# The first pair of modulation channels computed one block of 128 at a time, with the first key and value products between the two

## The chip, the cores and the metric

The kernel runs on one core of a Trainium2 chip. The metric is device time in microseconds (us) of one execution. TensorE (PE in the profile) multiplies and transposes, VectorE (DVE) and ScalarE (ACT) do elementwise work, GpSimd (POOL) a few small powers, and SyncE (SP) issues most of the loads.

## The reference

Two layers run over 256 latent tokens `x` and 256 context tokens `ctx`, each token 2048 channels wide. What matters here is how the first layer begins:

```python
shift, scale, gate = adaln(c, ada_w[i], ada_b[i])        # silu(c) @ w + b, in three
h  = modulate(rms_norm(x, norm_g[i]), shift[:, None], scale[:, None])
shift_c, scale_c, gate_c = adaln(c_ctx, ada_w[i], ada_b[i])
hc = modulate(rms_norm(ctx, norm_g[i]), shift_c, scale_c)   # h * (1 + scale) + shift
...
p  = h @ w_in                                            # queries, keys, values, ...
pc = hc @ w_in[:, base:]
```

So the first projection needs, for each channel, a scale and a shift that come from a matrix-vector product with `ada_w` (2048 rows), and the normalised tokens with the channel on the partitions. Attention, a state-space scan, an output projection and a second layer follow; the change does not touch them.

## The kernel before

Everything stays in float32 accuracy by splitting operands in a high and a low part: each product of a token block with a weight block is three matmuls (high by high, low by high, high by low). `hH[kb]` and `hL[kb]` are the high and low part of the modulated tokens for channel block `kb` (128 channels, 512 tokens: x in the first 256, ctx in the others); there are 16 such blocks. `w0` holds the weights of keys, values and queries in segments of 256 channels by 512 columns, 512 KB each. A weight segment lands in a `raw` buffer, ACT casts it to its high part, DVE subtracts to make the low part.

The first projection runs over eight pairs of channel blocks, `j` = 0 to 7. For each pair:

- `ada_gen` makes the scale (`A0`) and the shift (`S0`) of its 256 channels. Each needs four 512 KB blocks of `ada0` (512 rows by 256 columns each). PE multiplies them with `cpad`, which holds the two conditioning vectors in 32 columns, so that four row groups can stand in four strips of a PSUM bank (`32 * g`). ACT copies the bank to `half` (L724), PE turns it (L199), DVE sums the strips (L732) and adds the bias (L735, L736, L738).
- Then ACT makes `hH` (L757) and DVE a full-precision copy (L759) and from it `hL` (L763).
- The main loop multiplies: K and V for four token tiles of 128, Q for two, and one further block of 256 columns (`b_part`).

The tokens come in rows: `x_load(t)` loads tile t in two transfers (L583), `x_norm` squares, sums and scales it (L601, L603, L613, L615), `x_pair` turns two channel blocks by four transposes of 128 by 128 (L199) and copies them out on ACT and DVE (L628, L629) to `xm`. Tiles 0 and 1 are x, tiles 2 and 3 ctx. Tile 2 is loaded into the buffer of tile 0 (tag `KT`) and tile 3 into that of tile 1 (tag `KL`).

Order is set twice. Loads go through one list (`loads`) in the order in which it was filled, each as soon as a buffer is free, all on SP's queue: nine 512 KB buffers at the start. Instructions are recorded by a planner: `ada_gen`, `x_gen(0)` and `x_gen(1)` are generators that yield what they wait for, `pump` and `force` take the one that the planner's own clock finds ready, and the main loop calls them between its matmuls. Each engine then runs its instructions in the order of recording. For `j` = 0 the weights of K are split by halves of 128 channels (`split_half`, L440 and L443), and the main loop runs K for both token tiles of x, channel block 0 first, then V, then Q, and the ctx tiles 2 and 3 after them.

```python
q_ada(0)                 # 8 blocks: scale and shift of channel blocks 0 and 1
w_seg(0, CK, CV, CQ)     # K, V, Q weights of the pair
loads.append(lambda: x_load(2))
loads.append(lambda: x_load(3))
```

Of the kernel before, what the change touches and what calls it, by code (L numbers as in the profile page):

```python
# [14 lines left out]
D = 2048  # L15
# [126 lines left out]
def kernel(ctx: ExitStack, tc, x, cx, ada0, w0, adaT, w_in, w_out, sc_in, sc_out, rpb, small, const,  # L142
# [12 lines left out]
    def st(shape, tag, dt=F32, name=None):  # L155
        return sb.tile(list(shape), dt, tag=tag, name=name or tag, bufs=1)
# [15 lines left out]


    xrow = [st([128, D], "KT", name="x0")]
    QT, Vt, gt = st([128, 4, 256], "QT", F32R), st([128, 4, 512], "Vt"), st([128, 4, 256], "gt")
    xrow.append(st([128, D], "KL", name="x1"))
    QL = st([128, 4, 256], "QL", F32R)
# [219 lines left out]
    def place():  # L397
        in_use.append(free_w.popleft())
        return in_use[-1]
# [36 lines left out]
    def split_half(b):  # L436

        raw, v = RAW[0]
        H, Lo = (w[0].rearrange("p (b c) -> p b c", b=2) for w in (WH, WL))
        E(S.copy(H[:, b], v[:, b]))  # L440

        def rest():
            E(V.tensor_tensor(out=Lo[:, b], in0=v[:, b], in1=H[:, b].bitcast(F32), op=ALU.subtract))  # L443
            if b:
                RAW.pop(0)
                place()
                HL[0] = (H, Lo)
                pos["split"] += 1
                give_raw(raw)
                issue()  # L450

        halfsplit.append(rest)

# [79 lines left out]
    loads.append(lambda: E(DMA.dma_start(sm[:, NFIRST:], small[:, NFIRST:])))  # L533
    loads.append(lambda: E(DMA.dma_start(cs_[:, CFIRST:], const[:, CFIRST:])))
    weight(w_in, 0, 2, COL_B, 256)
    q_ada(1)
    for j in range(1, 8):
        w_seg(j, CK, CV)
        if j < 7:
            q_ada(j + 1)  # L540
        w_seg(j, CQ)
        weight(w_in, j * 256, 2, COL_B, 256)
    loads.append(later_loads)

    order = list(range(0, 6)) + list(range(8, 16)) + [6, 7]
# [32 lines left out]
    def x_load(t):  # L578
        src = x if t < 2 else cx
        r0 = (t % 2) * 128  # L580
        xt = xrow[t] if t < 2 else st([128, D], ("KT", "KL")[t % 2], name=f"x{t}")
        for q in range(0, 4, 2):
            E(DMA.dma_start(xt[:, q * 512:(q + 2) * 512], src[r0:r0 + 128, q * 512:(q + 2) * 512]))  # L583
            XS[4 * t + q], XS[4 * t + q + 1] = (xt[:, p * 512:(p + 1) * 512] for p in (q, q + 1))

    x_load(0)
    x_load(1)
# [112 lines left out]
    need = [0]  # L700

    def ada_gen():
        bc = lambda ap: ap.unsqueeze(2).to_broadcast([128, 2, 2])
        for j in range(8):
            k2 = slice(2 * j, 2 * j + 2)
            for part, dst in ((0, A0), (1, S0)):
                ps = None
                for q in range(4):
                    key = ("ada", j, part, q)
                    w_ = 2 if j == 0 else 4  # L710
                    if q % w_ == 0:
                        ks = [("ada", j, part, q + i) for i in range(w_)]
                        yield when(lambda: all(k in RAW for k in ks))
                        yield W_("PE", *[RAW[k][1] for k in ks], nb=0 if ps is not None else 1)
                    if ps is None:
                        ps = bank()
                    raw, v = RAW.pop(key)
                    for g in range(4):
                        mm(ps[32 * g:32 * g + 32, :256], cpad[:, 4 * q + g, :], v[:, g, :], q == 0, q == 3)
                    give_raw(raw)  # L720
                    issue()
                yield W_("ACT", ps)
                Rt = half()
                E(S.copy(Rt, ps[:, :256]))  # L724

                yield W_("PE", Rt)
                for b in range(2):
                    turn(ps[:, 256 + b * 128:384 + b * 128], Rt[:, b * 128:(b + 1) * 128])
                give(free_h, Rt)
                yield W_("DVE", ps)  # L730
                p2 = dst[:, k2, :]
                E(V.tensor_reduce(out=p2, in_=ps[:, 256:].rearrange("p (b g c) -> p b c g", b=2, c=32)[:, :, 0:2, :],  # L732
                                  axis=AX.X, op=ALU.add))
                if part == 0:
                    E(V.tensor_tensor(out=dst[:, k2, :], in0=p2, in1=bc(bs1[:, k2]), op=ALU.add))  # L735
                    E(V.tensor_tensor(out=dst[:, k2, :], in0=dst[:, k2, :], in1=bc(g0[:, k2]), op=ALU.mult))  # L736
                else:
                    E(V.tensor_tensor(out=dst[:, k2, :], in0=p2, in1=bc(P_("ab0")[:, k2]), op=ALU.add))  # L738
                give(free_b, ps)

            for ts in ((0, 1), (2,), (3,)) if j == 0 else ((0, 1, 2, 3),):
                yield when(lambda: all(("xm", t, j) in got for t in ts))
                spans = [(k, slice(max(256 * k, 128 * ts[0]), min(256 * k + 256, 128 * ts[-1] + 128)))
                         for k in range(2) if {2 * k, 2 * k + 1} & set(ts)]
                o = slice(128 * ts[0], 128 * ts[-1] + 128)
                for kb in (2 * j, 2 * j + 1):
                    if j:

                        yield when(lambda: need[0] >= j or plan.t["DVE"] <= plan.t["PE"] + 600)
                    yield W_("DVE", xnT[kb][:, o])  # L750
                    hf = tmp()
                    if hH[kb] is None:
                        hH[kb] = st([128, 512], f"hH{kb}", F32R, name=f"hH{kb}")
                    if ts == (0, 1):
                        split_half(kb)
                    for k, ok_ in spans:
                        E(S.activation(hH[kb][:, ok_], xnT[kb][:, ok_], AF.Identity, scale=A0[:, kb, k:k + 1],  # L757
                                       bias=S0[:, kb, k:k + 1]))
                        E(V.tensor_scalar(out=hf[:, ok_], in0=xnT[kb][:, ok_], scalar1=A0[:, kb, k:k + 1],  # L759
                                          scalar2=S0[:, kb, k:k + 1], op0=ALU.mult, op1=ALU.add))  # L760
                    if hL[kb] is None:
                        hL[kb] = st([128, 512], f"hL{kb}", F32R, name=f"hL{kb}")
                    E(V.tensor_tensor(out=hL[kb][:, o], in0=hf[:, o], in1=hH[kb][:, o].bitcast(F32), op=ALU.subtract))  # L763
                    give(free_t, hf)
                    if ts == (0, 1):
                        halfsplit.pop()()
                if ts == (0, 1):
                    hold[0] = False
                    split()
                    split()  # L770
                got.update(("h", j, t) for t in ts)


    Bl, Cl = st([128, 2, 256], "Bl"), st([128, 2, 256], "Cl")
# [94 lines left out]

    for j in range(8):  # L870
        need[0] = j
        force(lambda: ("h", j, 0 if j == 0 else 3) in got, (urgent,))
        if j == 0:

            w3 = [use(k) for k in range(3)]
            psQ = banks(2)
            psk = banks(2)
            for k in range(2):

                for i, (a_, w_) in enumerate(((hH, 0), (hL, 0), (hH, 1))):  # L880
                    for t in range(2):
                        mm(psk[t], a_[k][:, t * 128:(t + 1) * 128], w3[0][w_][:, k], k == 0 and i == 0, k == 1 and i == 2)
            for t in range(2):
                spawn(urgent, part_gen(j, "K", t, parK[t], psk[t]))
            pump()
            for t in range(2):
                kv(j, "V", t, w3[1])
# [25 lines left out]
    force(lambda: all(("part", 7, key, t) in got for key in "KV" for t in range(4)), (urgent,))  # L913
    got.add(("V", 0))
    KT, KL = st([128, 4, 512], "KT", F32R), st([128, 4, 512], "KL", F32R)


    cwh = st([128, 160], "cwh")
# [1134 lines left out]
```

## Time and profile before

| what | us |
|---|---|
| median of three runs | 1763.31 |
| the runs | 1763.47, 1763.31, 1760.44 |
| profiled execution | 1760.31 |
| its span in the profile | 1758.5 |
| PE busy in the span | 1736.7 |
| DVE busy, ACT busy | 1223.6, 773.4 |

The profile is one execution. Its span runs from the first to the last recorded instruction; 1.8 us of the execution's own time lie around it. A matmul on float32 data (the transposes apart) stands in the trace as two instructions; those on split operands (fp32r) as one.

### The profile page before, as it was taken

Reading aid. Unit: us, or ns where it says so; the run is one execution under the profiler, and the core shown is the slowest. Engines: PE = TensorE matmul, PEld = TensorE weight load, DVE = VectorE, ACT = ScalarE, POOL = GpSimd, SP = SyncE. Lnnn points to the kernel's source line nnn. Section 1 sums busy time; section 2 is a strip of 40 time slices with the busy share of each in tenths; the row PEclk is TensorE's granted clock in tenths of the full one; section 3 lists DMA queues with packets and bytes.
Section 4 is the critical chain, followed back from the end, with each engine's and each line's share of the span. In section 5 each row is a group of like instructions: output and inputs, shape, how many; then the busy total and the mean of one; then the engine's idle time right before and its main releaser. Section 6 shows DMA issues by size and latency. Waiting matters only on the chain.

```text
span 1758.5 us, 25025 instructions
## 1 busy us (share of the span) xinstructions
PE 1736.7 (99%) x9451; PEld 1463.1 (83%) x9451; DVE 1223.6 (70%) x1978; ACT 773.4 (44%) x1330; POOL 31.6 (2%) x28
## 2 busy tenths in 40 slices
PE   6999999999999999999999999999999999999998
PEld 4777988889888889888888898888888888888887
DVE  5666887878685878686877787787668555555554
ACT  5333544445242436343435343564446444444442
POOL 0000100001000000000000000000000000000000
PEclk9999999999999999999999999999999999999999
DMA  9987644686756767656776557768767666666563
GB/s 362 342 307 258 209 143 138 183 246 191 234 165 195 219 205 227 210 175 210 220 213 193 166 185 255 246 221 284 274 222 228 195 188 192 192 191 188 190 208 121
DMA packets 202536, 377.66 MB, mean 215 GB/s; under 512 B 32384, under 2 KB 69040, under 8 KB 202416
## 3 DMA queue, kind: packets, MB, share of 16 engines
q1 hardware_dynamic: 195152, 369.49, 65.5%
q10 hardware_dynamic: 7264, 6.58, 1.1%
q8 instruction: 74, 1.21, 0.3%
q14 instruction: 46, 0.38, 0.1%
HBM read 370.62 MB, written 6.71 MB: 215 GB/s over the span
## 4 chain that ended last, share of the span: by engine, by line
PE 94%; DMA 2%; DVE 2%; issue 1%; ACT 0%; POOL 0%; SPq 0%; ACTq 0%; DVEq 0%; POOLq 0%
PE bank L195 91%; PE bank L199 3%; DMA tmp<-dram_csr 1%; DVE w L427 1%; DMA raw<-in_ada 0%; DMA tmp<-dram_exr 0%; DMA raw<-in_adaT 0%; DVE tmp L1235 0%; ACT w L420 0%; POOL statk L572 0%; DVE mix L1562 0%; SPq L583 0%; DVE raw L823 0%; DVE tmp L603 0%; DVE Vt L1012 0%
## 5 line engine op out<-in xcount | busy, mean ns | idle before, releaser
L420 ACT CAST w<-raw 128x1024 fp32r<-128x1024 f32 x343 | 359.5, 1049 | 530.4 <-PE bank L195 447.7
L427 DVE TENSOR_TENSOR w<-raw,w 128x1024 fp32r<-128x1024 f32 x343 | 416.6, 1217 | 231.4 <-ACT w L420 230.1
L195 PE MATMUL bank<-hH,w 128*128 128x256 f32 (+1 forms) x2064 | 488.0, 324 | 1.2 <-DVE w L427 1.1
L195 PE MATMUL bank<-w,hH 128*128 128x512 f32 x1280 | 407.4, 396 | 2.7 <-ACT hH L757 2.5
L195 PEld LDWEIGHTS bank<-hH,w 128*128 128x128 f32 x2064 | 344.7, 188 | 34.2 <-DVE w L427 2.1
L195 PE MATMUL bank<-hL,w 128*128 128x256 f32 (+1 forms) x1040 | 334.3, 321 | 0.0
L195 PEld LDWEIGHTS bank<-w,hH 128*128 128x128 f32 x1280 | 237.7, 189 | 54.4 <-issue 4.0
L195 PE MATMUL bank<-w,hL 128*128 128x512 f32 x640 | 249.9, 391 | 0.1
L195 PEld LDWEIGHTS bank<-hL,w 128*128 128x128 f32 x1040 | 196.3, 189 | 14.9
L195 PE MATMUL bank<-w,h 128*128 128x512 f32 x768 | 179.7, 390 | 0.0
L823 DVE CUSTOM_DVE_ANT_0 raw<-raw,csb 128x1024 f32<-128x1024 f32 x128 | 155.4, 1219 | 26.2 <-DMA raw<-in_adaT 24.0
L195 PEld LDWEIGHTS bank<-w,h 128*128 128x128 f32 x768 | 143.6, 188 | 29.6
L195 PEld LDWEIGHTS bank<-w,hL 128*128 128x128 f32 x640 | 120.5, 188 | 25.4 <-DVE hL L763 0.6
L195 PE MATMUL bank<-w,mix 128*128 128x512 f32 x588 | 138.3, 391 | 0.9 <-DVE w L427 0.9
L195 PEld LDWEIGHTS bank<-w,mix 128*128 128x128 f32 x588 | 109.5, 188 | 24.0 <-DVE w L427 1.3
L1235 DVE SCALAR_TENSOR_TENSOR tmp<-bank,cwh,tmp 128x508 f32<-128x508 f32 (+1 forms) x96 | 71.0, 744 | 1.8
L195 PE MATMUL bank<-KL,h 128*128 128x512 f32 x264 | 63.8, 389 | 0.0
L427 DVE TENSOR_TENSOR KL<-raw,KL 128x1024 fp32r<-128x1024 f32 x32 | 39.1, 1223 | 33.1 <-ACT KL L420 33.1
L427 DVE TENSOR_TENSOR wL<-raw,wH 128x1024 fp32r<-128x1024 f32 x31 | 37.9, 1224 | 33.5 <-ACT wH L420 33.4
L427 DVE TENSOR_TENSOR QL<-raw,QT 128x1024 fp32r<-128x1024 f32 x32 | 39.2, 1224 | 29.8 <-ACT QT L420 29.8
L195 PEld LDWEIGHTS bank<-KL,h 128*128 128x128 f32 x264 | 49.5, 188 | 10.2
L195 PE MATMUL bank<-QT,h 128*128 128x512 f32 x168 | 56.2, 391 | 0.0
(291 smaller groups left out, 1984.7 us busy)
## 6 DMA issues: line engine op xcount, KB each, us to landing
raw<-in_w_in SPq DMA_DIRECT2D x196, 512.0 KB, 3.9
raw<-in_adaT SPq DMA_DIRECT2D x128, 512.0 KB, 4.8
raw<-in_sc_in SPq DMA_DIRECT2D x128, 512.0 KB, 3.8
raw<-in_w_out SPq DMA_DIRECT2D x64, 512.0 KB, 5.0
raw<-in_ada SPq DMA_DIRECT2D x34, 512.0 KB, 6.9
raw<-in_sc_out SPq DMA_DIRECT2D x32, 512.0 KB, 4.1
PT<-in_ada SPq DMA_DIRECT2D x16, 512.0 KB, 6.9
raw<-in_w SPq DMA_DIRECT2D x16, 512.0 KB, 6.1
```

What stands on the lines that cost most here:

```text
L195: E(T.matmul(o, l, r, start=start, stop=stop, skip_group_check=True))
L199: E(T.transpose(o, i, ident if k == 128 else ident[:k, :k]))
L420: E(S.copy(H, v))
L427: E(V.tensor_tensor(out=Lo, in0=v, in1=H.bitcast(F32), op=ALU.subtract))
L823: E(V.tensor_tensor_reduce(out=raw, in0=raw, in1=csb, scale=1.0, scalar=0.0, op0=ALU.mult, op1=ALU.add, accum_out=gp[:, h, m:m + 1]))
L1235: E(V.scalar_tensor_tensor(out=do, in0=di, scalar=cwh[:, 32 * k + ch:32 * k + ch + 1], in1=do, op0=ALU.mult, op1=ALU.add))
```

## The change

1. `ada0` is repacked on the host for the first pair: eight blocks of 512 KB as before, each now 1024 rows by 128 columns. A scale or a shift of 128 channels then needs two blocks.
2. The load order becomes: four blocks for channel block 0, K and V weights, four blocks for channel block 1, Q weights, tiles 2 and 3. Two small loads (the rest of `small` and `const`) go from behind tile 3 to the end of the first projection's list.
3. `ada_gen` computes scale and shift of channel block 0 alone, makes its `hH`, `hL` and the first half of the K weights, and reports `("row", 0)`; then the same for channel block 1.
4. The main loop runs K and then V with channel block 0 for both token tiles of x, waits for channel block 1, and runs K and V with it. Q follows as before.
5. `x_gen(0)` turns the first two channel blocks of x and then waits until the first K products are recorded (`k0`) before it turns the other fourteen.
6. Tile 2 gets buffers of its own (`QT` and `QL`, not yet in use then). Tile 3 now waits for the buffer of tile 0.

In the recorded order of the changed kernel, PE's instructions from the first one on are: scale of block 0 (8 + 8 matmuls of 128 columns), 4 transposes, one turn, shift of block 0 (8 + 8), one turn, K with block 0 (6), 28 transposes, scale of block 1 (8 + 8), V with block 0 (6), one turn, shift of block 1 (8 + 8), one turn, a small turn, K and V with block 1 (12), Q (12), and then tile 2.

```diff
-    q_ada(0)
-    w_seg(0, CK, CV, CQ)
+    def q_ada_one(kb):
+        for part in range(2):
+            for q in range(2):
+                loads.append(("a", ("one", kb, part, q), ada0, 4 * kb + 2 * part + q, 8, 0, 128, 2))
+
+    q_ada_one(0)
+    w_seg(0, CK, CV)
+    q_ada_one(1)
+    w_seg(0, CQ)
     loads.append(lambda: x_load(2))
     loads.append(lambda: x_load(3))
-    loads.append(lambda: E(DMA.dma_start(sm[:, NFIRST:], small[:, NFIRST:])))
-    loads.append(lambda: E(DMA.dma_start(cs_[:, CFIRST:], const[:, CFIRST:])))
...
-        xt = xrow[t] if t < 2 else st([128, D], ("KT", "KL")[t % 2], name=f"x{t}")
+        xt = xrow[t] if t < 2 else None if t == 2 else st([128, D], "KT", name="x3")
...
         for k2 in range(c, KB // 2):
+            if k2 == 1 and not c:
+                yield when(lambda: "k0" in got)
             yield from x_pair(k2, ts)
...
+        def part_sum(part, kbs, keys, together):
+            n = 128 * len(kbs)
+            nb, ps = 1024 // n, None
+            for q in range(len(keys)):
...
+                for g in range(nb):
+                    ki = q * nb + g
+                    mm(ps[32 * (g % 4):32 * (g % 4) + 32, :n], cpad[:, ki, :], v[:, g, :], ki < 4, ki >= 12)
...
+        for kb in range(2):
+            for part in range(2):
+                yield from part_sum(part, (kb,), [("one", kb, part, q) for q in range(2)], 1)
+            yield both((0, 1), 0)
+            yield from rows_of(0, kb, (0, 1))
+            got.add(("row", kb))
+            if kb == 0:
+                split()
...
-        force(lambda: ("h", j, 0 if j == 0 else 3) in got, (urgent,))
+        force(lambda: ("h", j, 3) in got if j else ("row", 0) in got, (urgent,))
         if j == 0:
+            w3, pss0 = [], []
+            for k in range(2):
+                if k:
+                    force(lambda: ("h", 0, 1) in got, (urgent,))
+                for q, (key, par) in enumerate((("K", parK), ("V", parV))):
+                    if k == 0:
+                        w3.append(use(q))
+                        pss0.append(banks(2))
+                    for i, (a_, w_) in enumerate(((hH, 0), (hL, 0), (hH, 1))):
+                        for t in range(2):
+                            mm(pss0[q][t], a_[k][:, t * 128:(t + 1) * 128], w3[q][w_][:, k], k == 0 and i == 0, k == 1 and i == 2)
+                    got.add("k0")
+                    pump()
...
```

More of the change, by code (lines that the diff above doesn't have):

```diff
@@ L445, in rest @@
                 RAW.pop(0)
+                give_raw(raw)
+                issue()
+            else:
                 place()
@@ L542 @@
         weight(w_in, j * 256, 2, COL_B, 256)
+    loads.append(lambda: E(DMA.dma_start(sm[:, NFIRST:], small[:, NFIRST:])))
+    loads.append(lambda: E(DMA.dma_start(cs_[:, CFIRST:], const[:, CFIRST:])))
     loads.append(later_loads)
@@ L580, in x_load @@
         r0 = (t % 2) * 128
[L581 removed]
+        xt = xrow[t] if t < 2 else None if t == 2 else st([128, D], "KT", name="x3")
         for q in range(0, 4, 2):
[L583 to L584 removed]
+            xq = xhalf[q // 2] if xt is None else xt[:, q * 512:(q + 2) * 512]
+            E(DMA.dma_start(xq, src[r0:r0 + 128, q * 512:(q + 2) * 512]))
+            XS[4 * t + q], XS[4 * t + q + 1] = xq[:, :512], xq[:, 512:]
     x_load(0)
@@ L702, in ada_gen @@
     def ada_gen():
[L703 to L771, printed above, removed]
@@ new lines, in part_sum @@
+        def part_sum(part, kbs, keys, together):
+            n = 128 * len(kbs)
+            nb, ps = 1024 // n, None
+            for q in range(len(keys)):
+                if q % together == 0:
+                    ks = keys[q:q + together]
+                    yield when(lambda: all(k in RAW for k in ks))
+                    yield W_("PE", *[RAW[k][1] for k in ks], nb=0 if ps is not None else 1)
+                if ps is None:
+                    ps = bank()
+                raw, v = RAW.pop(keys[q])
+                for g in range(nb):
+                    ki = q * nb + g
+                    mm(ps[32 * (g % 4):32 * (g % 4) + 32, :n], cpad[:, ki, :], v[:, g, :], ki < 4, ki >= 12)
+                give_raw(raw)
+                issue()
+            yield W_("ACT", ps)
+            Rt = half()
+            E(S.copy(Rt[:, :n], ps[:, :n]))
+            yield W_("PE", Rt)
+            for b in range(len(kbs)):
+                turn(ps[:, 256 + b * 128:384 + b * 128], Rt[:, b * 128:(b + 1) * 128])
+            give(free_h, Rt)
+            yield W_("DVE", ps)
+            k2 = slice(kbs[0], kbs[-1] + 1)
+            dst = (S0 if part else A0)[:, k2, :]
+            bc = lambda ap: ap[:, k2].unsqueeze(2).to_broadcast([128, len(kbs), 2])
+            E(V.tensor_reduce(out=dst, in_=ps[:, 256:256 + n].rearrange("p (b g c) -> p b c g", b=len(kbs), c=32)[:, :, 0:2, :],
+                              axis=AX.X, op=ALU.add))
+            if part == 0:
+                E(V.tensor_tensor(out=dst, in0=dst, in1=bc(bs1), op=ALU.add))
+                E(V.tensor_tensor(out=dst, in0=dst, in1=bc(g0), op=ALU.mult))
+            else:
+                E(V.tensor_tensor(out=dst, in0=dst, in1=bc(P_("ab0")), op=ALU.add))
+            give(free_b, ps)
@@ new lines, in rows_of @@
+        def rows_of(j, kb, ts):
+            spans = [(k, slice(max(256 * k, 128 * ts[0]), min(256 * k + 256, 128 * ts[-1] + 128)))
+                     for k in range(2) if {2 * k, 2 * k + 1} & set(ts)]
+            o = slice(128 * ts[0], 128 * ts[-1] + 128)
+            if j:
+                yield when(lambda: need[0] >= j or plan.t["DVE"] <= plan.t["PE"] + 600)
+            yield W_("DVE", xnT[kb][:, o])
+            hf = tmp()
+            if hH[kb] is None:
+                hH[kb] = st([128, 512], f"hH{kb}", F32R, name=f"hH{kb}")
+            if ts == (0, 1):
+                split_half(kb)
+            for k, ok_ in spans:
+                E(S.activation(hH[kb][:, ok_], xnT[kb][:, ok_], AF.Identity, scale=A0[:, kb, k:k + 1],
+                               bias=S0[:, kb, k:k + 1]))
+                E(V.tensor_scalar(out=hf[:, ok_], in0=xnT[kb][:, ok_], scalar1=A0[:, kb, k:k + 1],
+                                  scalar2=S0[:, kb, k:k + 1], op0=ALU.mult, op1=ALU.add))
+            if hL[kb] is None:
+                hL[kb] = st([128, 512], f"hL{kb}", F32R, name=f"hL{kb}")
+            E(V.tensor_tensor(out=hL[kb][:, o], in0=hf[:, o], in1=hH[kb][:, o].bitcast(F32), op=ALU.subtract))
+            give(free_t, hf)
+            if ts == (0, 1):
+                halfsplit.pop()()
@@ new lines, in ada_gen @@
+        both = lambda ts, j: when(lambda: all(("xm", t, j) in got for t in ts))
+        for kb in range(2):
[6 more added lines that the diff above has]
+                split()
+        hold[0] = False
+        split()
+        got.update(("h", 0, t) for t in (0, 1))
+        for t in (2, 3):
+            yield both((t,), 0)
+            for kb in range(2):
+                yield from rows_of(0, kb, (t,))
+            got.add(("h", 0, t))
@@ L774 @@
+        for j in range(1, 8):
+            for part in range(2):
+                yield from part_sum(part, (2 * j, 2 * j + 1), [("ada", j, part, q) for q in range(4)], 4)
+            yield both((0, 1, 2, 3), j)
+            for kb in (2 * j, 2 * j + 1):
+                yield from rows_of(j, kb, (0, 1, 2, 3))
+            got.update(("h", j, t) for t in range(4))
     Bl, Cl = st([128, 2, 256], "Bl"), st([128, 2, 256], "Cl")
@@ L2028 @@
                      for j in range(8) for b in (2048, 0) for q in range(4)]).reshape(64, 128, 1024)
+    for kb in range(2):
+        for part, b in enumerate((2048, 0)):
+            for q in range(2):
+                w = f('ada_w')[0][q * 1024:(q + 1) * 1024, b + kb * 128:b + kb * 128 + 128]
+                ada0[4 * kb + 2 * part + q] = w.reshape(8, 128, 128).transpose(1, 0, 2).reshape(128, 1024)
     w0 = np.stack([f('na_ssd_w_in')[0][j * 256:j * 256 + 256, c:c + 512].reshape(2, 128, 512).transpose(1, 0, 2)
```

24 lines of the change are left out of this document (9 added, 15 removed).

## The prediction

> **What bounds the kernel now.** I read the page's head first, then what PE waited for after the first 40 us, then PE's busy time and granted clock in stretches (columns of a stretch: its bounds, its length, PE busy and instructions, clock, DMA share, GB/s).
>
> ```profile
> span 1758.5 us, 25025 instructions
> PE 1736.7 (99%) x9451; PEld 1463.1 (83%) x9451; DVE 1223.6 (70%) x1978; ACT 773.4 (44%) x1330; POOL 31.6 (2%) x28
> ```
>
> ```profile
> PE bank L195 <- DVE w L427: 2.0, 3, 0.9
> PE bank L199 <- POOL r L1664: 0.3, 1, 0.3
> PE bank L195 <- DVE gt L789: 0.2, 1, 0.2
> ```
>
> ```profile
> 17.39:21.23 3.84, 3.31 (x51) 1.00 1.03 410
> 21.23:24.64 3.41, 1.84 (x8) 1.00 1.03 406
> 24.64:28.05 3.41, 3.41 (x9) 0.50 1.02 403
> 28.05:31.46 3.41, 3.41 (x16) 1.00 1.06 395
> 31.46:34.87 3.41, 2.32 (x12) 1.00 1.03 406
> 34.87:38.28 3.41, 3.06 (x12) 1.00 1.03 412
> ```
>
> After 40 us PE waits 2.5 us in 1718. Whatever comes after the start is a fixed amount of PE work, and the recorded order of the changed kernel is the same there apart from the first few pairs. So the change is worth what it moves the moment at which PE goes over to unbroken work. In the stretches up to 24.64 PE is idle for 0.53 and 1.57 us, and from 24.64 to 28.05 it runs at half clock, which loses half of 3.41, 1.7 us. These 3.8 us are all that lies between the first transposes and the last matmul of queries, so no more than this can be won. DMA runs at about 400 GB/s all the while, but the next rows show that PE, not a landing, sets this stretch.
>
> ```profile
> 10.82 2.28 PE L195 MATMUL bank<-raw,cpad 128*32 128x256 f32 x16 [10.82 <-DMA raw<-in_ada]
> 13.03 4.36 PE L199 MATMUL bank<-const,x 128*128 128x128 f32 x32
> 17.32 1.07 PE L195 MATMUL bank<-raw,cpad 128*32 128x256 f32 x16
> 20.57 0.61 PE L195 MATMUL bank<-xtm,cpad 128*32 128x256 f32 x8
> 23.35 0.74 PE L195 MATMUL bank<-w,hH 128*128 128x512 f32 x2 [1.11 <-ACT hH L757]
> ```
>
> ```profile
> 12.02 0.20 PEld L195 LDWEIGHTS bank<-raw,cpad 128*32 128x32 f32 x8 [0.99 <-DMA raw<-in_ada]
> 10.00:15.00 5.00, 4.06 (x28) 2.40 (x29) 2.12 (x7) 2.88 (x8) 0.56 (x1) 1.00 1.03 417
> ```
>
> The first two blocks of the scale are waited for (10.82 and 12.02). At 417 GB/s a block of 524288 bytes takes 1.26 us, so block n lands at about 10.8 + 1.26 (n - 1). By then PE is in the 32 transposes, and from 17.32 on it finds its blocks there. The last shift matmul ends at 20.57 + 0.61 = 21.18, the first K matmul starts at 23.35.
>
> ```profile
> 23.35 10.21 PE bank L195 x36
> 33.56 0.23 PE bank L199 x2
> ```
>
> This is the chain of waits. K, V and Q of the x tiles, 36 matmuls, take 10.21 us and end at 33.56; tile 2 follows. 33.56 is the mark that I compare.
>
> **The change, step by step.** The new order is worked through from 13.03, where the first four transposes start in both.
>
> *Up to the first K.* Shift of channel block 0 needs block 4: 10.8 + 3 x 1.26 = 14.6, and half of the 1.07 us that two blocks took, 15.15. From there the way to K is that of before, 23.35 - 21.18 = 2.17:
>
> ```profile
> 21.25 0.37 ACT L724 COPY half<-bank 128x256 f32<-128x256 f32 x1 [2.42 <-PE bank L195]
> 21.68 0.44 PE L199 MATMUL bank<-const,half 128*128 128x128 f32 x2 [0.49 <-ACT half L724]
> 23.33 0.43 DVE L763 TENSOR_TENSOR hL<-tmp,hH 128x256 fp32r<-128x256 f32 x1 [0.28 <-ACT hH L757]
> 23.67 0.68 DVE L443 TENSOR_TENSOR w<-yi,w 128x512 fp32r<-128x512 f32 x1
> 28.38 0.63 PE L195 MATMUL bank<-w,hH 128*128 128x512 f32 x2
> 33.17 0.39 PE L195 MATMUL bank<-w,hH 128*128 128x512 f32 x1
> 33.81 0.27 ACT L628 COPY xm<-bank 128x128 f32<-128x128 f32 x1 [1.58 <-PE bank L199]
> ```
>
> The copy is half as wide (0.27 for 0.37) and one turn of the two falls away, so 2.0: K starts at 17.15, 6.2 us before now. Its weights are block 5, 15.85, and their cast fits in before `hH`. K's last two matmuls want the low part of the weights, which ends 1.0 us after K's first start (23.67 + 0.68 - 23.35). A matmul costs 0.228 us (21 start between 28.38 and 33.17, with the clock at 1.00 but for the first instants), so K with block 0 ends at 17.15 + 1.0 + 0.45 = 18.6.
>
> *The 28 transposes that now follow.* On ACT and DVE their copies go so:
>
> ```profile
> 14.81 2.99 ACT L628 COPY xm<-bank 128x256 f32<-128x256 f32 x7 [0.25 <-PE bank L199]
> 15.21 3.05 DVE L629 COPY xm<-bank 128x256 f32<-128x256 f32 x7 [0.20 <-ACT xm L628]
> 25.73 2.35 DVE L427 TENSOR_TENSOR w<-raw,w 128x1024 fp32r<-128x1024 f32 x2
> ```
>
> At 4.36 / 32 = 0.136 each they take 3.8 us, to 22.4; the lower bound is the pace of the copies, seven pairs in 3.0. Before, they filled the time in which the blocks of the scale landed; now they stand on PE ahead of channel block 1, whose blocks 7 to 10 land at 18.4 to 22.15.
>
> *Channel block 1.* Scale 1.07, to 23.5. V with block 0: four matmuls to 24.4; its low part stands on DVE behind the seven copies, which end 0.87 after PE's transposes (15.21 + 3.05 - 17.39), so 23.3, and takes 1.2 (2.35 for two): 24.5, V ends 24.95. A turn (0.2) and the shift (1.07): 26.2. Again 2.0 to K: 28.2, with PE idle but for a turn; nothing is left to fill this gap, the transposes being done. K with block 1 to 28.2 + 1.0 + 0.45 = 29.65, V 6 x 0.228, Q 12 x 0.228: 33.75. Against 33.56 that is +0.2, at full clock throughout, where before carries a stretch at half clock. So 12 matmuls are brought forward, but 2.5 us of holes are new: before K, 14 to 17 us, the transposes are gone.
>
> *Tile 2 does not go ahead of this.* Its path now:
>
> ```profile
> 28.00 0.68 DVE L603 CUSTOM_DVE_ANT_0 tmp<-x 128x512 f32<-128x512 f32 x1
> 29.22 0.08 DVE L603 DVE_READ_ACCUMULATOR2_ANT ssq<- 128x1 f32 x1
> 30.42 0.72 ACT L613 ACTIVATE x<-x,rx 128x512 f32<-128x512 f32 x1 [0.32 <-POOL rx L572]
> ```
>
> Two sums take 1.3 (28.00 to 29.30), another 1.1 passes to the scaling at 30.42, which takes 0.72. In the new order the sums still stand on DVE behind the low part of Q's weights: 29.2 + 1.2 + 1.3 + 1.1 + 0.72 = 33.5, just before Q's end. From there to tile 2's K it is the path of now, and tile 3's sums come behind it on DVE, so the shift is handed on whole.
>
> *The narrow matmuls.* The trace has none of 32 columns on 128. Twice as many instructions with half the data:
>
> ```profile
> L195 PE MATMUL bank<-raw,cpad 128*32 128x256 f32 x272 | 18.8, 397 | 10.9 <-DMA raw<-in_ada 10.8
> L195 PE MATMUL bank<-tmp,xtm 128*64 128x128 f32 x128 | 8.8, 279 | 0.0
> L199 PE MATMUL bank<-const,tmp 128*128 128x128 f32 x356 | 50.5, 272 | 0.0
> ```
>
> 256 long in 32 columns costs 69 ns an instruction (18.8 / 272). 128 long costs 142 in 128 columns and 69 in 64; if it goes on falling with the strips it is 35 in 32, also half of the first row and the low end. If an instruction has a floor there, it is 69, the high end. I take 35. Scale and shift of channel block 1 are 64 such instructions on the path: 2.2 us for the 2.14 that I counted, +0.1; at the high end 4.4, +2.3.
>
> *The loads.* Tile 3 waits for the last transpose of x and is issued near 22.5; tile 2 is issued without a wait.
>
> ```profile
> 19.68 0.33 SPq L533 DMA_DIRECT2D small<-in_small x1
> 38.82 0.87 PE bank L199 x6
> 160.72 0.42 SPq L381 DMA_DIRECT2D raw<-in_adaT x1
> L919 DVE TENSOR_SCALAR cwh<-small x1: 237/237/237, 197.3 to 197.3; 128x160 f32<-128x160 f32 x1
> ```
>
> The queue behind it holds the `w_in` block and the next pair's eight `ada0` blocks; what was issued before lasts until block 13, 25.9, so DMA does not run dry, and tile 3 lands near 28.5. Its first transpose is at 38.82: 10 us of cover. If that were gone, each us of lateness would count. The eight blocks land by about 39 (28.5 + 0.6 + 8 x 1.26), and PE takes the first of them only behind that transpose. The two small loads move from 19.68 to about 160, ahead of the first `adaT` load; their first reader is at 197.3. I put the loads at nothing.
>
> *The clock.* The only stretch of the quoted table with less than 2 us of PE work in 3.41 us (1.84) is followed by one at 0.50; 2.32 was followed by 1.00. In the new order 14.4 to 17.8 holds two blocks' shift matmuls, two turns and the start of K, about 1.7 to 2; and the 2 us gap before K with block 1 makes a second such stretch. Both are followed by dense work, where half clock costs 1.7. Zero to two of these: 0 to 3.4. I take two, by the row that is nearest.
>
> The Trainium skill (TensorE: Matmul & The Clock Gate, "What's actually happening") has PE fall back to half rate after about 3.4 us idle, and recover after as long a busy stretch. By that rule neither gap would halve the clock and the sum would be +0.3. The trace agrees with the length (3.41 at 0.50), not with the condition: the longest wait ahead of it was 1.11.
>
> **Sum.** +0.2 order, +0.1 narrow matmuls, +3.4 clock = +3.7. Against the profiled execution (1758.5 span and 1.8 around it, 1760.31) that gives 1764.0. Two of the three runs lie 3 us above the profiled one; set on the median, 1763.31 + 3.7 = 1767.0.
>
> **Rivals.**
> - The clock stays full, and the transposes run at the copies' pace (3.0 for 3.8): 0.3 - 0.8 = -0.5, 1762.8. Not slower; it decides if the gaps before both K's fall across two clock stretches. For it: 2.32 of 3.41 did not halve. Against it: 1.84 did.
> - One stretch at half clock: 0.3 + 1.7 = +2.0, 1765.3. For it: the same pattern before. Against it: there are now two gaps.
> - The narrow matmuls have a floor of 69 ns: 2.2 more than my value, +5.9, 1769.2. For it: no row shows fewer ns than 69 for a float32 matmul. Against it: 142 and 69 in the rows.
> - Faster: the transposes vanish from the path of channel block 1, which is then bounded by block 10: 22.15 + 0.55 + 2.0 = 24.7 for K, 3.5 earlier; 33.75 - 3.5 = 30.25, 3.3 less than now, 1760.0. The recorded order speaks against it.
>
> **How the numbers follow.** Forecast 0.38, of which 0.28 above 0.2% (3.5 us; that is what a measurement of this kernel can tell from no change); one stretch 0.15 (0.03 above); full clock 0.23; floor 0.17, all above; faster 0.07: its 3.3 is just short of the 3.5, and more would have to come from a place that I don't see. Slower 0.28 + 0.03 + 0.17 = 0.48, same 0.10 + 0.12 + 0.23 = 0.45, faster 0.07. The range goes from 1761, full clock with the median 2 us towards the lower run, to 1770.5, floor and clock with 1.6 for a copy or load that I put at nothing.
>
> **What would show it.** K's first matmul near 17; transposes near 18.6 to 22.4; a gap of PE before K with channel block 1 near 26 to 28; two stretches at 0.50; 64 narrow instructions in 2.2 us; Q's end at 34 to 37.5; PE unbroken after 40. Wrong, if channel block 1's K starts by 25, if the clock is full throughout, or if tile 3 is waited for.

## The result and the profile after

| kernel | median us | runs | lowest to highest |
|---|---|---|---|
| before | 1763.39 | 6 | 1759.93 to 1765.2 |
| after | 1773.51 | 6 | 1770.39 to 1778.11 |

The ratio is 1.0063, 95% interval 1.0044 to 1.0081: the change makes the kernel 8 to 14 us slower. The profiled execution of after took 1770.39, the shortest of its six; its span is 10.1 longer than that of before.

The page's head and what PE waited for after the first 40 us (waits: total, times, longest), in after:

```profile
span 1768.6 us, 25153 instructions
PE 1739.7 (98%) x9515; PEld 1464.3 (83%) x9515; DVE 1225.0 (69%) x1983; ACT 773.4 (44%) x1332; POOL 31.7 (2%) x28
...
PE bank L196 <- DVE w L428: 5.7, 4, 3.5
PE bank L196 <- DVE hL L773: 1.7, 1, 1.7
PE bank L196 <- ACT hH L767: 0.7, 1, 0.7
```

Before had 2.5 us of such waits, after has 8.9 (the three rows and 0.8 in three smaller ones). Three of them are new: 3.5, 1.7 and 0.7. The start is not where the time went. PE's first 35 us in after (timeline: start, length, instruction):

```profile
14.28 1.94 PE L196 MATMUL bank<-raw,cpad 128*32 128x128 f32 x32
...
18.22 0.73 PE L196 MATMUL bank<-w,hH 128*128 128x512 f32 x2 [1.15 <-ACT hH L767]
...
19.86 3.22 PE L200 MATMUL bank<-const,x 128*128 128x128 f32 x28
...
25.90 0.64 PE L196 MATMUL bank<-yi,cpad 128*32 128x128 f32 x16
26.36 0.62 PE L196 MATMUL bank<-raw,cpad 128*32 128x128 f32 x16
...
34.50 0.38 PE L200 MATMUL bank<-const,x2a 128*128 128x128 f32 x2
```

Tile 2's first transposes, which stand right behind Q in both kernels, come at 34.50. The same instructions in before, and then a mark further on that both kernels have, the wait for `gt`:

```profile
33.40 0.38 PE L199 MATMUL bank<-const,x 128*128 128x128 f32 x2
87.89 0.50 PE L195 MATMUL bank<-w,hH 128*128 128x512 f32 x1 [0.22 <-DVE gt L789]
```

```profile
94.83 0.50 PE L196 MATMUL bank<-w,hH 128*128 128x512 f32 x1 [0.23 <-DVE gt L819]
```

So 1.1 us is lost by the end of Q (0.8 of it is PE's pace in the first 16 us of this execution, see the last section), and 6.9 by 94.83: 5.8 us go between. They go at pair `j` = 1. After there, PE, ACT, DVE in turn:

```profile
57.62 0.91 PE L196 MATMUL bank<-w,hH 128*128 128x512 f32 x2 [3.54 <-DVE w L428]
```

```profile
49.70 0.37 ACT L734 COPY half<-bank 128x256 f32<-128x256 f32 x1 [2.00 <-PE bank L196]
51.26 1.09 ACT L767 ACTIVATE hH<-xm,S,A 128x256 fp32r<-128x256 f32 x2 [1.19 <-DVE S L750]
52.26 1.04 ACT L421 CAST w<-raw 128x1024 fp32r<-128x1024 f32 x1
53.20 1.04 ACT L421 CAST w<-PT 128x1024 fp32r<-128x1024 f32 x1
...
54.62 1.09 ACT L767 ACTIVATE hH<-xm,S,A 128x256 fp32r<-128x256 f32 x2
```

```profile
55.74 0.69 DVE L773 TENSOR_TENSOR hL<-tmp,hH 128x512 fp32r<-128x512 f32 x1 [2.02 <-ACT hH L767]
56.35 1.22 DVE L428 TENSOR_TENSOR w<-raw,w 128x1024 fp32r<-128x1024 f32 x1
```

Read from the end: PE's third matmul wants the low part of the weights, made by DVE at 56.35. DVE had its input since ACT's cast at 52.26 + 1.04, but stands in its own order behind `hL` of the pair's second block, which wants `hH` of 54.62, and on ACT that `hH` stands behind two casts and a copy. The first cast is K's own, and PE's first matmul of the pair uses it at 53.35. The second is for V, which comes later, while the `hH` behind it was needed next. Before, the same stretch of ACT reads:

```profile
44.73 0.37 ACT L724 COPY half<-bank 128x256 f32<-128x256 f32 x1 [2.18 <-PE bank L195]
...
46.47 1.09 ACT L757 ACTIVATE hH<-xm,S,A 128x256 fp32r<-128x256 f32 x2 [0.82 <-DVE S L738]
...
49.25 1.11 ACT L757 ACTIVATE hH<-xm,S,A 128x256 fp32r<-128x256 f32 x2
50.25 2.00 ACT L420 CAST w<-raw 128x1024 fp32r<-128x1024 f32 x2
```

Both `hH` were ahead of both casts, and the shift (`half`) of the pair was done 5 us sooner. For PE's own order has turned here too: in after the 32 matmuls of that shift (47.70 to 49.64) stand behind tile 3's K (from 45.45), in before ahead of it (42.72 to 44.66, K from 46.53). Which of the two turns costs the time, the first experiment tells. Behind the new wait of after the clock falls (stretches: bounds, length, PE busy, and further on the granted clock, DMA share and GB/s):

```profile
54.56:57.97 3.41, 0.35 (x2) 0.31 (x3) 2.23 (x3) 1.15 (x3) 0.00 (x0) 1.00 0.85 346
57.97:61.38 3.41, 3.41 (x24) 1.59 (x26) 1.42 (x2) 0.00 (x0) 0.00 (x0) 0.51 0.71 233
```

3.54 of wait and half of 3.41 are 5.2 of the 5.8. The other two waits are at the last pair, `j` = 7. PE, then ACT, in after:

```profile
187.29 0.51 PE L196 MATMUL bank<-w,hH 128*128 128x512 f32 x1 [0.73 <-ACT hH L767]
189.50 0.50 PE L196 MATMUL bank<-w,hL 128*128 128x512 f32 x1 [1.70 <-DVE hL L773]
```

```profile
185.69 1.05 ACT L421 CAST w<-raw 128x1024 fp32r<-128x1024 f32 x1 [1.66 <-PE bank L196]
186.65 1.09 ACT L767 ACTIVATE hH<-xm,S,A 128x256 fp32r<-128x256 f32 x2
```

Again a cast stands ahead of an `hH`, and the cast itself waited 1.66 us for PE. PE is busy 7.57 of the 10 us from 180 to 190, where before it was busy for all 10: 2.4 us. The sum so far, 1.1 + 5.8 + 2.4 = 9.3 of 10.1. The other 0.8 is a balance of later places, among them a wait of 1.07 at 248.39 that before doesn't have, and one of 0.9 between 1100 and 1200 that after doesn't have.

### The profile page after: what moved, and what is told of

It is laid out like the page before. It is cut to its first block, busy times and chain, and to the rows that moved or that the text cites. A ratio compares the mean times of both kernels' runs of the same rounds, so it can differ in the third digit from the quotient of the medians.

```text
span 1768.6 us, 25153 instructions
## 1 busy us (share of the span) xinstructions
PE 1739.7 (98%) x9515; PEld 1464.3 (83%) x9515; DVE 1225.0 (69%) x1983; ACT 773.4 (44%) x1332; POOL 31.7 (2%) x28
## 4 chain that ended last, share of the span: by engine, by line
PE 95%; DVE 2%; DMA 1%; ACT 1%; issue 1%; POOL 0%; SPq 0%; DVEq 0%; POOLq 0%; ACTq 0%
PE bank L196 92%; PE bank L200 3%; DVE w L428 1%; DMA raw<-in_ada 0%; ACT w L421 0%; DMA raw<-in_sc_in 0%; DVE tmp L1272 0%; POOL statk L581 0%; ACT hH L767 0%; DVE hL L773 0%; DVE tmp L769 0%; DVE tmp L613 0%; SPq L593 0%; DVE tmp L1012 0%; DVE KL L428 0%
## 5 line engine op out<-in xcount | busy, mean ns | idle before, releaser
L853 DVE CUSTOM_DVE_ANT_0 raw<-raw,csb 128x1024 f32<-128x1024 f32 x128 | 155.3, 1218 | 30.0 <-DMA raw<-in_adaT 27.5
```

The costliest lines, as they stand in the source:

```text
L853: E(V.tensor_tensor_reduce(out=raw, in0=raw, in1=csb, scale=1.0, scalar=0.0, op0=ALU.mult, op1=ALU.add, accum_out=gp[:, h, m:m + 1]))
```

## The experiments

Two theories stood after these profiles. One: the recorded order at pairs 1 and 7, which turned with the change, costs the time. The other: data come late (tile 3 has to wait for a buffer, the load list is longer at its front), or the halves and the held transposes are the loss. All ratios are against runs of before on the same chip.

| run | what | median us | ratio | interval |
|---|---|---|---|---|
| e1_pair1 | after, `hH` of pair 1 forced earlier | 1768.44 | 1.0031 | 1.0020 to 1.0042 |
| e2_pair1_pair7 | the same, and pair 7 too | 1763.77 | 1.0005 | 0.9994 to 1.0015 |
| e3_no_hold | after, transposes not held | 1775.08 | 1.0059 | 1.0046 to 1.0072 |
| e4_own_buffer | after, tile 3 in a buffer of its own | 1771.96 | 1.0045 | 1.0032 to 1.0058 |
| e6_fill2 | e2, transposes spread over the holes | 1763.98 | 1.0006 | 0.9994 to 1.0017 |
| e7_fill3 | e2, spread otherwise, tile 3's own buffer | 1763.41 | 1.0014 | 1.0003 to 1.0025 |
| o1_tail | after, the two small loads where they were | 1763.55 | 0.9996 | 0.9981 to 1.0010 |
| b1_before_small_last | before, only the two small loads moved | 1772.17 | 1.0049 | 1.0034 to 1.0064 |

**Forcing the order.** The main loop asks the planner for the rows of pair 1 ahead of tile 3's V, and in e2 also for those of pair 7 ahead of pair 6's Q. Loads and computation stay those of after.

```diff
                 for key, k in (("K", 0), ("V", 1)):
+                    if t == 3 and k == 1:
+                        need[0] = 1
+                        force(lambda: ("h", 1, 3) in got, (urgent,))
                     kv(j, key, t, w3[k])
...
             for key in "KVQ":
+                if j == 6 and key == "Q":
+                    need[0] = 7
+                    force(lambda: ("h", 7, 3) in got, (urgent,))
```

The first part alone is e1_pair1:

> The changed kernel, with one thing put back: scale, shift and modulation of the second channel pair are recorded ahead of V of the last ctx tile, so that on ACT both `hH` of that pair stand ahead of the two weight casts for its K and V. Theory (order): PE's 3.5 us wait near 54 us and the half-clock stretch behind it (1.7) go, span 1768.6 - 5.3 = about 1763; the 2.4 us wait near 187 us stays. Rival (data): the wait is for weights that land late, since DMA fell to 4 to 128 GB/s between 39 and 43 us; then PE still waits 3 us or more near 54 and the span stays within 1 us of 1768. Rival (clock): what costs is how often the clock halves; then the wait goes but the time changes by no more than the 1.7.

Both parts:

> As e1_pair1, and the modulation of the eighth pair is recorded ahead of Q of the seventh, so that its second `hH` stands on ACT ahead of the casts that wait for PE. Theory (order): the waits of 0.7 and 1.7 us near 187 and 189 us go too, 2.4 us less than e1_pair1, span about 1761. What is then left against the span of before, 1758.5, is the 1.1 us of the first 35 us and some waits on weights between 200 and 300 us. Rival: the wait at the eighth pair is taken up by another one behind it (the casts of its weights come later on ACT), and e2 ties with e1.

In e1 the wait at pair 1 is 0.40, in after it was 3.54; the two at pair 7 stay. The shift matmuls still stand behind tile 3's K (47.54 to 49.48), so it is ACT's order of `hH` and casts that cost the 3.54:

```profile
55.37 0.73 PE L196 MATMUL bank<-w,hH 128*128 128x512 f32 x2 [0.40 <-DVE w L428]
```

The span did not fall to the 1763 that was expected, but to 1766.6. By pair 7 this execution is 2.6 us ahead of after (184.66 for 187.29, the first wait there). The forced order has small waits of its own (0.49 at 49.97, 0.52 at 71.74), and the start, which is that of after, holds a stretch at half clock that after's profile doesn't have (last section).

In e2 all three are gone, and the time is that of before within 0.15%. The largest entry of PE's waits after 40 us in e2 (four others are 0.5 and less):

```profile
PE bank L196 <- DVE w L428: 1.9, 4, 0.8
```

The ratio falls from 1.0063 by 0.0032 and then by 0.0026, 5.6 and 4.6 us, each with an uncertainty of some 3 to 4 us by the intervals. How the loss divides between the two places is therefore not settled; together they account for all of it, since e2's interval reaches from 1.1 us below before to 2.6 above. What the halves do at the start can't be told from nothing.

**Not holding the transposes.**

```diff
-            if k2 == 1 and not c:
-                yield when(lambda: "k0" in got)
```

> The changed kernel without its fifth part: the 28 transposes of x follow the first four at once, as before the change; scale and shift by 128 channels, and K and V by halves, stay. Prediction's theory (the transposes on the way of channel block 1 cost what the early products win): the first K starts near 21 instead of 18.2, channel block 1's K near 26 instead of 28.8, Q ends 2 us earlier than 34.7. Rival (they only fill the holes before K): Q ends within 0.5 us of 34.7. For the loss near 54 us both hold that it stays or grows, because in this order both `hH` of the second pair stand behind the two casts: 3.5 to 5 us of PE waiting, and a half-clock stretch behind it.

The first K comes at 21.05 and channel block 1's at 29.90, as the 28 transposes now stand ahead of the first K. Neither theory on the start came true: Q ends at 35.80, neither 2 us before 34.7 nor within 0.5 of it. A stretch at half clock from 22.52 to 25.93, 1.7 us, is in that, which after doesn't have. The loss stays. Both `hH` of pair 1 now stand behind the casts, and PE waits 1.98 for `hL` at 57.61; ACT of e3:

```profile
52.58 1.05 ACT L421 CAST w<-raw 128x1024 fp32r<-128x1024 f32 x1
...
54.49 2.07 ACT L765 ACTIVATE hH<-xm,S,A 128x256 fp32r<-128x256 f32 x4
```

So the hold isn't what turns the order.

**Tile 3 in buffers of its own.** It is loaded in four pieces into buffers that `hH12` to `hH15` use later, and waits for no transpose.

```diff
+        if t == 3:
+            for q in range(4):
+                XS[12 + q] = st([128, 512], f"hH{12 + q}", name=f"x3{q}")
+                E(DMA.dma_start(XS[12 + q], src[r0:r0 + 128, q * 512:(q + 1) * 512]))
+            return
```

> The changed kernel with tile 3 loaded into four buffers that are not yet in use (the last four `hH`), in four transfers of 256 KB, so that it waits for nothing; PE's order is the same instruction for instruction. Theory (order): nothing changes beyond 1 us, PE still waits 3.5 us near 54 us, although the next pair's blocks are issued up to 7 us earlier. Rival (data): the wait near 54 us comes from loads that were held up behind tile 3; it shrinks by 2 us or more.

The longest waits are those of after, to the tenth:

```profile
PE bank L196 <- DVE w L428: 7.1, 5, 3.5
PE bank L196 <- DVE hL L778: 1.7, 1, 1.7
```

Tile 3's load is issued from 17.19 on, in after from 23.05, and the waits don't move: tile 3's lateness is not the cause. The test reaches less far than was expected of it, though. The blocks of pair 1 are issued from 25.01, in after from 25.07, and not up to 7 us earlier. These blocks as a cause are ruled out by e1, which keeps after's loads and loses the wait.

**Filling the holes.** With the order forced as in e2, the rest of the change should have had something to win: PE stands idle ahead of both K's while 28 transposes wait. e6 puts 12 of them behind the rows of channel block 0, 8 behind the first K, 8 behind the rows of block 1; e7 puts 12, 8 and 8 behind the rows of block 0, those of block 1 and Q, and gives tile 3 the buffers of e4.

```diff
             if k2 == 1 and not c:
+                yield when(lambda: ("row", 0) in got)
+            if k2 == 4 and not c:
                 yield when(lambda: "k0" in got)
+            if k2 == 6 and not c:
+                yield when(lambda: ("row", 1) in got)
```

> e2_pair1_pair7 with the 28 transposes split over the holes of PE: 12 of them recorded behind the turn that precedes K with channel block 0, 8 behind that K as in the change, 8 behind the turn that precedes K with channel block 1. Theory (the start is a matter of PE's order alone: transposes cost only where PE has other work): first K still near 17.5, channel block 1's K near 25.5 to 26 instead of 27.9, Q's end near 31.7 instead of 33.7, time 2 us less than e2_pair1_pair7, 1761.5 at the median, about 0.1% under before. Rival (copies): ACT and DVE copy each pair in 0.43 us and stand ahead of the cast and the low parts that K and V need; then channel block 1's K comes no earlier than 27.5 and e6 ties with e2_pair1_pair7.

> As e6_fill2, but no transpose of x is left on the way from the first K to channel block 1: 12 in the hole before the first K, 8 in the one before channel block 1's K, 8 behind Q, where PE waits for tile 2; tile 3 has buffers of its own as in e4_own_buffer, since tile 0's is free only then. Theory (order): channel block 1's K is bounded by its last block, 22.15 + 0.55 + 2.0, near 25; Q's end near 31 and tile 2's K near 33.5 instead of 35.45; time 2.5 to 3 us less than e2_pair1_pair7, 1761 at the median, 0.15% under before. Rival: tile 2's chain on DVE (two sums behind the low part of Q's weights) is what sets tile 2's K, which then stays within 1 us of e6_fill2, and the 8 transposes and their copies ahead of tile 2's only delay it.

Neither gained. Channel block 1's K starts at 27.06 in e6 (expected by 26, by the rival not before 27.5) and at 26.85 in e7 (expected near 25). In e6 PE comes to tile 2's K with time in hand, and stands there. PE in e2, then PE and ACT in e6:

```profile
35.45 0.51 PE L196 MATMUL bank<-w,hH 128*128 128x512 f32 x1 [1.39 <-ACT hH L767]
```

```profile
35.49 0.79 PE L196 MATMUL bank<-w,hH 128*128 128x512 f32 x1 [1.81 <-ACT hH L771]
```

```profile
32.47 0.72 ACT L623 ACTIVATE x2a<-x2a,rx 128x512 f32<-128x512 f32 x1 [1.30 <-POOL rx L581]
...
34.95 0.87 ACT L771 ACTIVATE hH<-xm,S,A 128x128 fp32r<-128x128 f32 x2
```

The time won by filling turns into 0.4 more of waiting for tile 2's `hH` (1.81 for 1.39), which ACT can't make before its scaling at 32.47 to 34.28, and into a stretch at half clock behind the wait (0.50 from 35.24 to 38.66). Tile 2's K starts at the same moment. In e7 it is 35.83 with a wait of 1.99, and half clock from 37.17 on. In both, the normalisation of tile 2 sets the end of the start, with a sum for tile 3 that stands on ACT ahead of the `hH` (34.33 to 34.97 in e6); PE doesn't.

**The two small loads.** What of the change turns the order? With the two small loads put back behind tile 3, and all else of the change in place, the recorded order of ACT has both `hH` of pair 1 ahead of the casts again, and both `hH` of pair 7 too. The other way round, moving nothing but these two loads in the kernel before puts the casts in front. (The expectations call pair 1 the second block and pair 7 block 8.)

```diff
     loads.append(lambda: x_load(3))
+    loads.append(lambda: E(DMA.dma_start(sm[:, NFIRST:], small[:, NFIRST:])))
+    loads.append(lambda: E(DMA.dma_start(cs_[:, CFIRST:], const[:, CFIRST:])))
     weight(w_in, 0, 2, COL_B, 256)
...
-    loads.append(lambda: E(DMA.dma_start(sm[:, NFIRST:], small[:, NFIRST:])))
-    loads.append(lambda: E(DMA.dma_start(cs_[:, CFIRST:], const[:, CFIRST:])))
     loads.append(later_loads)
```

> The kernel after with the two small loads put back behind tile 3's load; everything else of the change stays. The recorded order of ScalarE then has both hH of the second block ahead of the two weight casts of that block, and both hH of block 8 ahead of the casts of the next pair, as in the kernel before. If moving the two small loads is what turned the recorded order, the wait of 3.5 us at 54 us, the half clock behind it and the two waits at 187 to 190 us are gone, and the time is 1762 to 1767 us, where the run with both orders forced stood (1763.8). If the rest of the change (halves, held transposes) makes the waits, they stay and the time is 1770 to 1774 us.

The reverse, in the kernel before (the same two lines, moved from behind tile 3 to the end):

> The kernel before with nothing but the two small loads moved to the end of the list of loads, as the change has them. The recorded order of ScalarE then has both casts of the second block ahead of its first hH, and at block 8 an additional cast ahead of the first hH. If moving these loads is the cause by itself, PE waits 2 to 4 us for the second block near 50 us (and loses up to 1.7 us of clock behind it) and 1 to 3 us at block 8, and the time is 1766 to 1771 us. If the loads matter only together with the halves, or not at all, it is within 0.1% of before, 1762 to 1765 us.

Both came as the first theory has it: 0.9996 with the loads back, 1.0049 with the loads alone moved (b1's median, 1772.17, is 1.2 us above the range that was expected). The mark of `gt` comes at 88.72 in o1, 0.8 behind before, where after was 6.9 behind. ACT at pair 1 in o1, and PE's stretch there (12 of 12 busy, clock 1.00; after has 8.46 of 12 at 0.86):

```profile
47.32 1.10 ACT L767 ACTIVATE hH<-xm,S,A 128x256 fp32r<-128x256 f32 x2 [0.82 <-DVE S L750]
...
50.10 1.10 ACT L767 ACTIVATE hH<-xm,S,A 128x256 fp32r<-128x256 f32 x2
51.10 1.05 ACT L421 CAST w<-raw 128x1024 fp32r<-128x1024 f32 x1
```

```profile
50.00:62.00 12.00, 12.00 (x83) 8.46 (x85) 7.69 (x14) 3.95 (x7) 0.00 (x0) 1.00 1.03 401
180.00:190.00 10.00, 10.00 (x45) 8.26 (x44) 7.35 (x11) 1.23 (x2) 0.00 (x0) 1.00 0.63 194
```

And in b1, which has none of the halves, ACT at pair 1, PE there and at pair 7, and PE's stretches:

```profile
50.68 2.00 ACT L420 CAST w<-raw 128x1024 fp32r<-128x1024 f32 x2
52.58 2.08 ACT L757 ACTIVATE hH<-xm,S,A 128x256 fp32r<-128x256 f32 x4
```

```profile
55.71 0.80 PE L195 MATMUL bank<-w,hL 128*128 128x512 f32 x1 [1.98 <-DVE hL L763]
...
185.64 0.51 PE L195 MATMUL bank<-w,hH 128*128 128x512 f32 x1 [0.74 <-ACT hH L757]
187.84 0.50 PE L195 MATMUL bank<-w,hL 128*128 128x512 f32 x1 [1.70 <-DVE hL L763]
```

```profile
50.00:62.00 12.00, 9.64 (x64) 5.89 (x57) 5.99 (x11) 4.61 (x8) 0.00 (x0) 0.86 0.95 348
180.00:190.00 10.00, 7.57 (x29) 5.63 (x28) 8.14 (x12) 3.10 (x4) 0.00 (x0) 0.93 0.55 160
```

The waits at pair 7 are those of after, 0.73 and 1.70, in a kernel that has nothing else of the change; the clock falls there too in b1 (0.93 in the row), which it doesn't in the profile of after. So pair 7 costs 2.4 us where the clock stays up and 1.7 more where it falls. Whether that is why forcing pair 7 was worth 4.6 us between e1 and e2 isn't shown: in e1's own profile the clock doesn't fall there. Moving two loads is sufficient, and taking the move back is enough to undo the loss. The moved loads as such cost nothing: in e2 they are moved too, and with the order forced the time is that of before. The expectation for o1 of 1762 to 1767 held; its profiled run, 1767.25, is among the longest of its twelve, with 3.1 us of waits for casts of weights near 1125 us and a half-clock stretch behind them, far from the change.

Why the planner turned is read from the code, not from a run. A weight block is cast as soon as the planner's own clock has it landed, and `pump` tries the casts before the rows. Two loads fewer ahead of the weights change when these land in that clock. Which comparison tipped was not traced. No run beats before.

## Why the prediction was wrong

- **First K with channel block 0 at 17.15:** 17.38 in e2, 17.91 in o1, 18.22 in after, where the 32 shift matmuls took 1.94 and not the 1.07 that were counted. Right in kind, up to 1.1 late. In e1, with the same start, they took 1.08: in after and o1 PE still went at half its pace there (last section).
- **Transposes 18.6 to 22.4, lower bound 3.0:** 19.86 to 23.08, 3.22 us. That is PE's pace and not the copies': one starts every 0.11 us. The 0.136 of the prediction is a mean over before, where the first ones came every 0.21 and the others every 0.11.
- **Channel block 1's K at 28.2:** 27.94 in e2, 28.47 in o1, 28.78 in after, 29.30 in e1. The gap of PE before it is there: the shift ends at 26.98, and between there and 28.78 stand two turns.
- **End of Q at 33.75, +0.2:** 33.68 in e2, 34.20 in o1, 34.50 in after, 35.04 in e1 (tile 2's first transposes, right behind Q), against 33.40 for the same instruction before; +0.3 to +1.6. PE's order up to there is the same in these four, and what sets them apart is mostly PE's pace at the beginning and one stretch at half clock in e1. The reading that the order alone is about a wash held (+0.3 in e2).
- **Narrow matmuls at 35 ns:** 32 in 0.64 + 0.62 less the overlap, 25.90 to 26.98: 1.08 us, 34 ns each. The rival of a 69 ns floor falls.
- **Two stretches at half clock at the start:** none in after's profile, whose stretches from 10.57 to 34.87 all stand at 1.00; 14.4 to 17.8, for which 1.7 to 2 us of PE work were expected, holds 2.29. In e1's profile, which has the same start, there is one: 1.88 of 3.41 us busy, then 3.41 at half clock. So in these executions the term of +3.4 is 0 or 1.7, and the start stands at the edge between the two (last section). The one stretch at half clock in after came behind a wait that the prediction didn't have. The rival of full clock had the start as such cost or win nothing, 1762.8; the change without the moved loads measures 1763.55, 0.9996 of before.
- **Tile 2 doesn't go ahead, the shift is handed on whole:** it held. Tile 2's K starts at 36.28 in after and at 35.13 in before, 1.15 apart, as Q's end was 1.1. And where e6 and e7 freed PE, it stayed at 35.5 to 35.8.
- **The loads at nothing:** right for their own time (e2), wrong for what they turned. The prediction followed the two small loads on SP's queue up to their first reader at 197.3, and didn't follow that the planner decides by the list when casts are recorded.
- **The step that failed:** "Whatever comes after the start is a fixed amount of PE work, and the recorded order of the changed kernel is the same there apart from the first few pairs. So the change is worth what it moves the moment at which PE goes over to unbroken work." The amount of PE work is fixed; its unbroken run isn't. After 40 us PE waits 8.9 us in after, where "PE unbroken after 40" was to show that the prediction was right. The first few pairs were set aside without a price, pair 7 is not among the first few, and the order whose turn costs is that of ACT: one `hH` behind two casts costs 5.2 at pair 1, one behind a single cast 2.4 at pair 7. Neither was a rival.
- The forecast of slower was right in sign, but by luck: its +3.4 of clock at the start is 0 in after's profile, and the 8 us that are there come from pairs 1 and 7. (The upper end of the range, too, is 1769.2 + 1.6 = 1770.8 by its own sum, not 1770.5. The measured 1773.51 lies above both.)

## What to carry to other kernels

Where a planner records the order, each edit of what it plans with, a load list too, can turn the order far from the edit: compare the recorded order of every engine over all stages, not PE's and not the start alone, and look for work needed late that now stands ahead of work needed next. A one-microsecond cast ahead of a one-microsecond row cost 2.4 us here and two cost 5.2, since DVE stood still behind them and the clock fell after the wait. And to fill an idle engine is worth nothing until what ends the next wait (here tile 2's `hH` on ACT) comes sooner.

## What was not expected of the hardware

Half clock came behind the long wait. The wait is 3.54 us, the stretch around it has PE busy for 0.35 of 3.41 us, and the next stretch ran at 0.51. That agrees with the rule of the Trainium skill (TensorE: Matmul & The Clock Gate, "What's actually happening") of about 3.4 us idle. But a stretch with half of it busy can be followed by half clock as well: in before, 1.84 of 3.41. In the start of the changed kernel it goes either way. The first two rows are e1's, the third is e2's, which has the same order there and goes on at 1.00:

```profile
14.32:17.73 3.41, 1.88 (x36) 1.25 (x35) 2.02 (x9) 2.27 (x5) 0.00 (x0) 1.00 1.03 410
17.73:21.14 3.41, 3.41 (x14) 2.90 (x13) 0.56 (x2) 0.86 (x2) 0.00 (x0) 0.50 1.02 407
```

```profile
14.74:18.15 3.41, 1.87 (x32) 1.25 (x25) 2.09 (x9) 2.20 (x4) 0.00 (x0) 1.00 1.03 410
```

The half-clock stretches of one profile start whole multiples of 3.413 us apart (in b1 at 24.68, 55.40 and 188.52, 9 and 39 of them; every profile has one at its end, too), so a profile can be cut along them. Cut so, the ten profiles show this, from 10 us on to 20 us before the end: every stretch at full clock with PE busy for 1.61 us or less was followed by half clock, none with 1.91 or more was, and of eight between 1.71 and 1.88 four were. The old start lost 1.7 us to this in both of its profiles (before and b1). The new start lost them in e1 and not in after, e2, e4 and o1.

The column of the granted clock stands at 1.00 in the first 17 us as well, but PE's pace there says otherwise. The same length in after and in e1, both in the shift matmuls of channel block 0:

```profile
14.28:15.14 0.86, 0.86 (x18) 0.80 (x21) 0.53 (x3) 0.26 (x1) 0.00 (x0) 1.00 0.99 395
```

```profile
14.34:15.20 0.86, 0.86 (x33) 0.81 (x32) 0.53 (x3) 0.26 (x1) 0.00 (x0) 1.00 0.98 391
```

The one holds 18 of PE's instructions, the other 33. Four shift matmuls come every 0.21 us in after and o1, to the last of them at 15.79 and 15.62, and every 0.11 in e1. The transposes of before come every 0.21 us up to 14.37 and every 0.11 from 14.50 on. So PE begins at half pace, and when the full pace comes differs between executions. That is 0.8 us of the first K (18.22 in after, 17.38 in e2), and these 0.8 stand unchanged at the end of Q (34.50 and 33.68).
